# Loads of small parameters moved behind the weights of a decoder's first product

## The chip, the cores and the metric

The kernel runs on one NeuronCore of a Trainium2 chip. The metric is the device time of one execution in microseconds (us). Three timed runs of the kernel before gave 2286.88, 2286.91 and 2288.31 us, a median of 2286.91.

The engines are named as the profile names them: PE is TensorE, PEld its weight loads, ACT ScalarE, DVE VectorE, POOL GpSimd and SP SyncE, which here only asks for transfers (SPq is its queue of instructions). Each engine works through its instructions in their order: one that waits holds back all that stand behind it on that engine. A transfer is asked for by a DMA instruction on some engine; the data are moved by 16 DMA engines, and a semaphore tells the others when they have landed.

## The reference, cut to what matters

The model is a decoder of two layers for 256 tokens of width 2048, in float32. The first layer is an mLSTM mixer and a gated feed-forward block, the second an attention over shared keys and values and another feed-forward block. The part in question is the very start of layer 1:

```python
def rms_norm(x, g):
    xf = x.astype(jnp.float32)
    y = xf * lax.rsqrt(jnp.mean(xf * xf, axis=-1, keepdims=True) + EPS)
    return (y * g.astype(jnp.float32)).astype(x.dtype)
...
def mlstm_mixer(xn, w_in, b_igate, b_fgate, w_hnorm, w_out):
    """xn: normed stream (B,S,D). One combined projection -> q,k,v, output gate, input/forget gates."""
    B, S, _ = xn.shape
    proj = xn @ w_in
    q, k, v, o, ig, fg = jnp.split(proj, M_SPLITS, axis=-1)
...
            h = h + mlstm_mixer(rms_norm(h, a_norm[layer]), m_w_in[layer], m_b_igate[layer],
                                m_b_fgate[layer], m_w_hnorm[layer], m_w_out[layer])
```

`x` is 256 x 2048 and `w_in` is 2048 x 6160. The first 1024 columns of `w_in` give q; the k, v, output gate and gate columns follow. All other products of the model have the same form: 256 tokens against a large weight matrix that is read once.

## The kernel before, in words

Every product is done in three matmuls of a rounded format (fp32r): a float32 operand is split into a high part (a copy on ACT, rounded) and a low part (the difference, on DVE), and high x high, high x low and low x high are summed in PSUM. So every weight tile that lands costs one copy on ACT and one subtraction on DVE before PE can use it. Landed weights lie in one of four buffers (`raw`, RAW = 4), split weights in one of five (`w2`, HL = 5): the copy of a split tile must wait until PE is done with the tile five before it.

The first product, `first_product` (L448), makes q. It goes through the 2048 rows of the weights in 16 chunks of 128 rows, called chunk 0 to 15 here. Chunk k needs 128 x 1024 weights (512 KB) and the 128 columns of x that go with it, turned. A load of x (L458, 256 KB) brings two chunks' columns; the weights of chunks 0 to 3 come one by one (512 KB, L463), and of chunks 4 to 15 in pairs (1 MB). `norm_a.operands(k)` (L202) turns two chunks' columns of x with four PE transposes into one PSUM bank (L207), scales them by the norm's gain and splits them: the high part on ACT (L282), the low part on DVE (L283). These are the operands x_a of chunks k and k + 1. The split of the weights is L478 (ACT) and L479 (DVE), and the 24 matmuls of a chunk are L484. The sums of squares for the norm (L200, ACT) are taken of 512 columns at a time (`SQ_AT` says after which chunks), and the row scale is applied to the products afterwards.

Around it: the norm's gain is loaded and turned first (`columns`, L135 to 149). Eleven small loads of other parameters (L172) and two of gate biases (L174, L175) are asked for by `parameters_in`, which is called when a counter of work pieces has gone 10 on (`later`, L643), held behind the latest weight load by `tc.issue_after`. The convolution's parameters (L144) and rotary tables (L700, L702) belong to the feed-forward block and are written further down (L831 to 834), after most of the output product. All transfers are asked for by SP. After the first product come `gates()` (L510) and the k product (L387), and from there on weights of 1 MB follow each other.

The written order isn't the order that runs. The framework's scheduler places each engine's instructions by its own timeline, and may place a load that is written late far ahead; `tc.issue_after(i)` keeps what is inside it behind instruction i. Semaphores for landed transfers go round: there are eight of them (DMAHW0 to DMAHW7), taken in turn, so a DMA instruction first waits until the transfer eight before it has landed.

Of the kernel before, what the change touches and what calls it, by code (L numbers as in the profile page):

```python
# [19 lines left out]
P = 128  # L20
# [21 lines left out]
X_AT = (0, 2, 3, 5, 6, 8, 9)  # L42
SQ_AT = (3, 6, 9, 12)
CW = 256
# [22 lines left out]
def trunk(  # L67
# [66 lines left out]

    def columns(sources, name):  # L135

        n = sum(s.shape[0] for s in sources)
        cols = const.tile([P, n], F32, name=name)
        at = 0
        for s in sources:  # L140
            for r0 in range(0, s.shape[0], P):
                r = min(P, s.shape[0] - r0)
                rows = work.tile([P, P], F32, tag="rows", name="rows")
                nc.sync.dma_start(rows[:r], s[r0:r0 + r])  # L144
                ps = small_ps("cols_ps")
                pe.transpose(ps[:, :r], rows[:r, :], ident[:r, :r])
                dve.tensor_copy(cols[:, at:at + r], ps[:, :r])
                at += r
        return cols

    gain_a = columns([rows_of(a_norm[0])], "gain_a")
    gate_b = const.tile([40, 1], F32, name="gate_b")
# [15 lines left out]
    def parameter_loads():  # L168
        at = 0
        for a in (rows_of(kv_norm), rows_of(b_norm[0]), rows_of(f_norm[0]), rows_of(f_norm[1]), rows_of(final_norm),  # L170
                  rows_of(m_w_hnorm[0].rearrange("h v -> (h v)")), rows_of(subln[0]), lam_q1, lam_k1, lam_q2, lam_k2):
            nc.sync.dma_start(rows[at:at + a.shape[0]], a)  # L172
            at += a.shape[0]
        nc.sync.dma_start(gate_b[0:8], m_b_igate.rearrange("o h -> h o"))  # L174
        nc.sync.dma_start(gate_b[32:40], m_b_fgate.rearrange("o h -> h o"))  # L175

# [271 lines left out]
    def first_product(evac):  # L448
# [10 lines left out]

        def w_in(k, kc):  # L460
            if k % 2 == 0:
                raw[0] = wpool.tile([P, 2, HQK], F32, tag="raw", name="raw", bufs=RAW)
            loads.append(nc.sync.dma_start(raw[0][:, k % 2:k % 2 + kc], w[k * P:(k + kc) * P, :HQK].rearrange("(k p) n -> p k n", p=P)))  # L463

        x_in(0)
        for k in range(KD):
            if k < 4:
                w_in(k, 1)
            elif k % 2 == 0:
                w_in(k, 2)  # L470
            if k in X_AT:
                x_in(2 + 2 * X_AT.index(k))
            if k % 2 == 0:
                norm_a.operands(k)
            part = raw[0][:, k % 2]
            w2 = wpool.tile([P, 2, HQK], F32R, tag="w2", name="w2", bufs=HL)
            for c in ((slice(0, 512), slice(512, HQK)) if k < 2 else (slice(0, HQK),)):
                act.activation(w2[:, 0, c], part[:, c], AF.Copy)  # L478
                dve.tensor_tensor(w2[:, 1, c], part[:, c], w2[:, 0, c].bitcast(F32), op=ALU.subtract)  # L479
            xh, xl, _ = xs[k]  # L480
            for j in range(n):
                s = slice(j * P, (j + 1) * P)
                for o, (a, b) in enumerate(((w2[:, 0, s], xh), (w2[:, 0, s], xl), (w2[:, 1, s], xh))):
                    pe.matmul(ps[j], a, b, start=(k == 0 and o == 0 and j % 2 == 0), stop=(k == KD - 1 and o == 2), skip_group_check=True)  # L484
            if k + 1 in SQ_AT:
# [7 lines left out]
    def mlstm(norm):  # L493
# [148 lines left out]

        later(10, parameters_in)  # L643
        later(13, parameters)
        first_product(evac_q)
# [184 lines left out]
    convs = []  # L830
    for layer in range(2):  # L831
        cw = columns([rows_of(conv_w[layer, 0]), rows_of(conv_w[layer, 1]), rows_of(conv_w[layer, 2]), rows_of(conv_b[layer])], f"conv{layer}")
        convs.append(cw.rearrange("p (j f) -> p j f", j=4))
    tables = rotary_tables()
    neg_lam = lambda_col()
# [97 lines left out]
```

## Time and profile before

| | us |
|---|---|
| median of three timed runs | 2286.91 |
| profiled execution, its own time | 2288.57 |
| its span, first to last instruction | 2286.8 |
| first matmul of the first product (L484) starts | 8.92 |
| first matmul of the k product (L387) starts | 67.31 |
| PE busy in the span | 2272.3 (99%) |

The profiled execution is 1.77 us longer than its span, and 1.66 us longer than the median of the timed runs. PE is busy nearly the whole time, and the chain of work that ended last is 98% PE. The stretches where PE does not work all lie in the first 36 us.

### The profile page before, as it was taken

Reading aid. Unit: us, or ns where it says so; the run is one execution under the profiler, and the core shown is the slowest. Engines: PE = TensorE matmul, PEld = TensorE weight load, DVE = VectorE, ACT = ScalarE, POOL = GpSimd, SP = SyncE. Lnnn points to the kernel's source line nnn. Section 1 sums busy time; section 2 is a strip of 40 time slices with the busy share of each in tenths; the row PEclk is TensorE's granted clock in tenths of the full one; section 3 lists DMA queues with packets and bytes.
Section 4 is the critical chain, followed back from the end, with each engine's and each line's share of the span. In section 5 each row is a group of like instructions: output and inputs, shape, how many; then the busy total and the mean of one; then the engine's idle time right before and its main releaser. Section 6 shows DMA issues by size and latency. Waiting matters only on the chain.

```text
span 2286.8 us, 31046 instructions
## 1 busy us (share of the span) xinstructions
PE 2272.3 (99%) x12034; PEld 1937.2 (85%) x12034; DVE 1516.2 (66%) x2445; ACT 1209.0 (53%) x1840; POOL 111.2 (5%) x305
## 2 busy tenths in 40 slices
PE   8999999999999999999999999999999999999998
PEld 8878888888888888888888888888888888888887
DVE  5755556777764577775588875557777545777754
ACT  5455554655553455554454556556565434555543
POOL 0013100000000000000022102200000000000000
PEclk9999999999999999999999999999999999999999
DMA  7554555555555555555556555555555555555553
GB/s 255 173 167 160 171 184 185 181 192 186 184 193 184 194 184 187 191 184 193 181 183 188 165 164 168 166 184 185 184 185 190 179 191 195 190 192 188 193 186 118
DMA packets 325192, 418.88 MB, mean 183 GB/s; under 512 B 9054, under 2 KB 238772, under 8 KB 325044
## 3 DMA queue, kind: packets, MB, share of 16 engines
q1 hardware_dynamic: 325044, 416.90, 55.1%
q8 instruction: 94, 1.54, 0.3%
q14 instruction: 54, 0.44, 0.1%
HBM read 414.77 MB, written 2.10 MB: 182 GB/s over the span
## 4 chain that ended last, share of the span: by engine, by line
PE 98%; DMA 1%; SPq 0%; DVE 0%; ACT 0%; issue 0%; DVEq 0%; ACTq 0%
PE acc L387 53%; PE acc L413 40%; PE acc L484 1%; PE val_ps L311 1%; PE acc L431 1%; DMA raw<-in_m_w_in_dram 1%; PE turn_ps L207 0%; DMA stream<-in_x_dram 0%; PE as_ps L768 0%; PE w_ps L593 0%; PE gps L510 0%; PE as_ps L769 0%; PE an_ps L333 0%; PE hn_ps L333 0%; PE s_ps L600 0%; SPq L463 0%
## 5 line engine op out<-in xcount | busy, mean ns | idle before, releaser
L353 DVE TENSOR_TENSOR w<-raw,w 128x1024 fp32r<-128x1024 f32 x768 | 938.6, 1222 | 620.6 <-ACT w L352 619.4
L352 ACT ACTIVATE w<-raw 128x1024 fp32r<-128x1024 f32 x768 | 813.3, 1059 | 790.3 <-PE acc L413 396.1
L387 PE MATMUL acc<-x_f,w 128*128 128x512 f32 (+1 forms) x5632 | 987.5, 337 | 0.0
L387 PEld LDWEIGHTS acc<-x_f,w 128*128 128x128 f32 x5632 | 862.6, 188 | 122.5
L413 PE MATMUL acc<-w,hid 128*128 128x512 f32 (+1 forms) x2112 | 477.7, 388 | 0.0
L413 PEld LDWEIGHTS acc<-w,hid 128*128 128x128 f32 x2112 | 387.3, 188 | 87.5
L413 PE MATMUL acc<-w,x_a 128*128 128x512 f32 x768 | 183.3, 396 | 0.0
L387 PE MATMUL acc<-x_at,w 128*128 128x256 f32 (+1 forms) x1024 | 181.9, 338 | 0.0
L387 PEld LDWEIGHTS acc<-x_at,w 128*128 128x128 f32 x1024 | 156.8, 188 | 22.1
L413 PEld LDWEIGHTS acc<-w,x_a 128*128 128x128 f32 x768 | 142.7, 188 | 32.7
L393 ACT ACTIVATE low<-acc 128x256 f32<-128x256 f32 x216 | 79.5, 385 | 147.2 <-PE acc L387 147.2
L394 DVE TENSOR_TENSOR acc<-acc,low 128x256 f32<-128x256 f32 x216 | 84.8, 432 | 52.2 <-ACT low L393 52.1
L667 ACT ACTIVATE c<-u,conv 128x256 f32<-128x256 f32 x176 | 95.9, 592 | 0.2 <-DVE u L665 0.2
L413 PE MATMUL acc<-w,ao 128*128 128x512 f32 x384 | 92.2, 397 | 0.0
L752 POOL TENSOR_TENSOR sw<-sw,sin_t 32x256 f32<-32x256 f32 x32 | 40.6, 1280 | 1059.7 <-DVE sw L751 1044.6
L413 PE MATMUL acc<-w,x_at 128*128 128x512 f32 x384 | 91.9, 396 | 0.0
L413 PE MATMUL acc<-w,mo 128*128 128x512 f32 x384 | 91.3, 397 | 0.0
L413 PEld LDWEIGHTS acc<-w,mo 128*128 128x128 f32 x384 | 71.4, 188 | 16.5
L413 PEld LDWEIGHTS acc<-w,ao 128*128 128x128 f32 x384 | 71.4, 188 | 16.3
L413 PEld LDWEIGHTS acc<-w,x_at 128*128 128x128 f32 x384 | 71.3, 188 | 16.1
L668 DVE SCALAR_TENSOR_TENSOR c<-u,conv,c 128x255 f32<-128x255 f32 x176 | 77.0, 478 | 0.0
L669 DVE SCALAR_TENSOR_TENSOR c<-u,conv,c 128x254 f32<-128x254 f32 x176 | 76.8, 477 | 0.1
(239 smaller groups left out, 1166.9 us busy)
## 6 DMA issues: line engine op xcount, KB each, us to landing
raw<-in_w_up_dram SPq DMA_DIRECT2D x176, 1024.0 KB
raw<-in_w_down_dram SPq DMA_DIRECT2D x79, 1024.0 KB
raw<-in_m_w_in_dram SPq DMA_DIRECT2D x46, 1024.0 KB
raw<-in_w_kv_dram SPq DMA_DIRECT2D x32, 1024.0 KB
raw<-in_m_w_out_dram SPq DMA_DIRECT2D x16, 1024.0 KB
raw<-in_w_q_dram SPq DMA_DIRECT2D x16, 1024.0 KB
raw<-in_w_o_dram SPq DMA_DIRECT2D x16, 1024.0 KB
raw<-in_w_down_dram SPq DMA_DIRECT2D x15, 512.0 KB
```

The source lines that it names most:

```text
L311: pe.matmul(ps[:, :vh.shape[1]], a, b, start=(s == 0 and o == 0), stop=(s == t and o == 2))
L352: act.activation(w2[:, :hc, 0], part, AF.Copy)
L353: dve.tensor_tensor(w2[:, :hc, 1], part, w2[:, :hc, 0].bitcast(F32), op=ALU.subtract)
L387: pe.matmul(to, a, b, start=(k == 0 and o == 0), stop=(k == kn - 1 and o == len(ops) - 1))
L393: act.activation(low, p[:, T:], AF.Copy)
L394: dve.tensor_tensor(p[:, :T], p[:, :T], low, op=ALU.add)
L413: pe.matmul(ps[t], a[:, s], b, start=(k == 0 and o == 0), stop=(k == kn - 1 and o == 2))
L431: pe.matmul(ps[t], a[:, s], b, start=(k == 0 and o == 0), stop=(k == kn - 1 and o == 2))
L667: act.activation(c, u, AF.Identity, bias=cw[:, 3, f:f + 1], scale=cw[:, 2, f:f + 1])
L668: dve.scalar_tensor_tensor(c[:, 1:], u[:, :T - 1], cw[:, 1, f:f + 1], c[:, 1:], op0=ALU.mult, op1=ALU.add)
L669: dve.scalar_tensor_tensor(c[:, 2:], u[:, :T - 2], cw[:, 0, f:f + 1], c[:, 2:], op0=ALU.mult, op1=ALU.add)
L752: pool.tensor_tensor(sw, sw, sin_t, op=ALU.mult)
```

## The change

Five edits. The gain of the first norm and the weights of chunk 0 are asked for on ACT's queue instead of SP's, the weights in two halves of 512 columns. The four transposes of chunks k and k + 1 are kept behind the last matmul of chunk k - 2. The sums of squares are written after chunks 6, 8, 10 and 12 instead of 3, 6, 9 and 12. The eleven parameter loads go from piece 10 to piece 20 and their transpose from 13 to 25; the two gate biases are apart from them, at piece 11. The convolution's loads and the rotary tables are kept behind the latest weight load. The amount of computation is the same.

```diff
-SQ_AT = (3, 6, 9, 12)
+SQ_AT = (6, 8, 10, 12)
...
-    def columns(sources, name):
+    def columns(sources, name, dma=None):
...
-                nc.sync.dma_start(rows[:r], s[r0:r0 + r])
+                (dma or nc.sync).dma_start(rows[:r], s[r0:r0 + r])
...
-    gain_a = columns([rows_of(a_norm[0])], "gain_a")
+    gain_a = columns([rows_of(a_norm[0])], "gain_a", nc.scalar)
...
+    def gate_biases_in():
+        with tc.issue_after(loads[-1].ins):
+            nc.sync.dma_start(gate_b[0:8], m_b_igate.rearrange("o h -> h o"))
+            nc.sync.dma_start(gate_b[32:40], m_b_fgate.rearrange("o h -> h o"))
...
+        halves = (slice(0, 512), slice(512, HQK))
+        for k in range(KD):
...
+            if k == 0:
+                for c in halves:
+                    w_in(k, 1, nc.scalar, c)
+            elif k < 4:
+                w_in(k, 1, nc.sync)
...
-            if k % 2 == 0:
+            if k == 0:
                 norm_a.operands(k)
+            elif k % 2 == 0:
+                with tc.issue_after(lasts[k - 2].ins):
+                    norm_a.operands(k)
...
+                    last = pe.matmul(ps[j], a, b, start=(k == 0 and o == 0 and j % 2 == 0), stop=(k == KD - 1 and o == 2), skip_group_check=True)
+            lasts.append(last)
...
-        later(10, parameters_in)
-        later(13, parameters)
+        later(11, gate_biases_in)
+        later(20, parameters_in)
+        later(25, parameters)
...
+    with tc.issue_after(loads[-1].ins):
+        for layer in range(2):
+            cw = columns([rows_of(conv_w[layer, 0]), rows_of(conv_w[layer, 1]), rows_of(conv_w[layer, 2]), rows_of(conv_b[layer])], f"conv{layer}")
+            convs.append(cw.rearrange("p (j f) -> p j f", j=4))
+        tables = rotary_tables()
```

What the scheduler makes of it is read from the order of instructions, at three places. A row is line, operation, what it writes <- what it reads, and the size. The lines of the changed kernel are 3 to 14 higher than those of the kernel before (L200 is L203 there, L207 is L210, L282 is L285, L478 is L489, L484 is L495).

The first is the start of ACT. w_169 is the split weights of chunk 0 before, w_199 of chunk 1; in the changed kernel they are w_170 and w_200. Before:

```order
L478 ACT_TABLE_LOAD
L478 ACTIVATE w_169<-raw 128x512 [waits DMAHW2_49]
L478 ACTIVATE w_169<-raw 128x512
L282 ACTIVATE x_a_163<-turn_ps,gain_a 128x256 [waits DVE_49,PE_49]
L200 ACTIVATE sq,parts_a<-stream 128x512 [waits DMAHW3_49,DMAHW1_49]
L200 ACTIVATE sq,parts_a<-stream 128x512
```

In the changed kernel, where DMAHW1 and DMAHW2 are the first two loads of x and DMAHW3 is the first half of chunk 0's weights:

```order
L144 DMA rows<-in_a_norm_dram 16x128
L464 DMA raw<-in_m_w_in_dram 128x512 x2
L203 ACT_TABLE_LOAD [waits DMAHW2_49]
L203 ACTIVATE sq,parts_a<-stream 128x512 [waits DMAHW1_49]
L203 ACTIVATE sq,parts_a<-stream 128x512
L489 ACTIVATE w_170<-raw 128x512 [waits DMAHW3_49]
L285 ACTIVATE x_a_164<-turn_ps,gain_a 128x256 [waits DVE_49,PE_49]
```

The sums of squares over the first two loads of x now stand ahead of the copy of chunk 0's first weights, and a wait for the second load of x stands ahead of ACT's table load.

The second place is SP, from the last three loads of x to the end of the first product's weights. Before:

```order
L458 DMA stream<-in_x_dram 128x2x256 x3
L144 DMA rows<-in_conv_w_dram 88x128 x2
L702 DMA fr<-in_freq_dram 32x2
L463 DMA raw<-in_m_w_in_dram 128x2x1024
L172 DMA rows<-in_kv_norm_dram 16x128
L172 DMA rows<-in_b_norm_dram 16x128
...
L174 DMA gate_b<-in_m_b_igate_dram 8x1
L175 DMA gate_b<-in_m_b_fgate_dram 8x1
L463 DMA raw<-in_m_w_in_dram 128x2x1024 x3
```

In the changed kernel:

```order
L461 DMA stream<-in_x_dram 128x2x256 x3
L464 DMA raw<-in_m_w_in_dram 128x2x1024 x2
L177 DMA gate_b<-in_m_b_igate_dram 8x1
L178 DMA gate_b<-in_m_b_fgate_dram 8x1
L464 DMA raw<-in_m_w_in_dram 128x2x1024 x2
L516 DMA gw<-in_m_w_in_dram 128x16x16
L346 DMA raw<-in_m_w_in_dram 128x8x256 x2
L172 DMA rows<-in_kv_norm_dram 16x128
L172 DMA rows<-in_b_norm_dram 16x128
```

The sixteen small loads that stood between the weights of chunks 6 and 7 and those of chunks 10 and 11 are gone from there; the eleven of L172 stand behind the second load of the k product.

The third place is chunk 10, on PE and on ACT. In the changed kernel x_a_454, x_a_523 and x_a_613 are the operands of chunks 9, 10 and 12, w_529 is the split weights of chunk 10 and w_697 those of chunk 14. On PE:

```order
L495 MATMUL acc<-x_a_454,w_485 128x256 x24
L210 MATMUL turn_ps<-ident,stream 128x128 x4
L495 MATMUL acc<-x_a_523,w_529 128x256 x24
L210 MATMUL turn_ps<-ident,stream 128x128
```

On ACT of the changed kernel:

```order
L489 ACTIVATE w_619<-raw 128x1024
L489 ACTIVATE w_657<-raw 128x1024
L489 ACTIVATE w_697<-raw 128x1024
L285 ACTIVATE x_a_523<-turn_ps,gain_a 128x256
L285 ACTIVATE x_a_526<-turn_ps,gain_a 128x256
```

On ACT of the kernel before, where w_541 is the split weights of chunk 10 and x_a_385 the operand of chunk 7:

```order
L282 ACTIVATE x_a_382<-turn_ps,gain_a 128x256
L478 ACTIVATE w_541<-raw 128x1024
L282 ACTIVATE x_a_385<-turn_ps,gain_a 128x256
L282 ACTIVATE x_a_450<-turn_ps,gain_a 128x256
```

Before, the operand of chunk 7 stood on ACT behind the copy of chunk 10's weights. In the changed kernel the transposes of chunk 10 stand directly ahead of its matmuls, and its operand stands on ACT behind the copy of chunk 14's weights, which takes the buffer of chunk 9's.

## Rows read from the trace of the kernel before

**Rows 1.** The page: busy time and share of each engine, part 1.

```profile
PE 2272.3 (99%) x12034; PEld 1937.2 (85%) x12034; DVE 1516.2 (66%) x2445; ACT 1209.0 (53%) x1840; POOL 111.2 (5%) x305
```

**Rows 2.** The chain of waits from 0 to 200 us: start us, us, what.

```profile
24.82 0.23 SPq L172
...
26.74 6.04 DMA raw<-in_m_w_in_dram
...
67.31 30.29 PE acc L387 x173
```

**Rows 3.** Timeline of PE: start us, us, engine, line, operation xcount [idle before, releaser].

```profile
8.50 0.66 PE L207 MATMUL turn_ps<-ident,stream 128*128 128x128 f32 x4 [3.04 <-DMA stream<-in_x_dram]
8.92 5.08 PE L484 MATMUL acc<-x_a,w 128*128 128x256 f32 x28
...
17.62 10.67 PE L484 MATMUL acc<-x_a,w 128*128 128x256 f32 x88
28.13 1.80 PE L207 MATMUL turn_ps<-ident,stream 128*128 128x128 f32 x15
...
34.34 0.74 PE L484 MATMUL acc<-x_a,w 128*128 128x256 f32 x4 [1.68 <-ACT x_a L282]
35.70 0.50 PE L484 MATMUL acc<-x_a,w 128*128 128x256 f32 x2 [0.62 <-DVE x_a L283]
```

**Rows 4.** Timeline of ACT, 3.9 to 36 us.

```profile
6.73 1.15 ACT L478 ACTIVATE w<-raw 128x512 fp32r<-128x512 f32 x2 [4.74 <-DMA raw<-in_m_w_in_dram]
...
8.54 0.63 ACT L200 ACTIVATE sq<-stream 128x512 bf16<-128x512 f32 x1 [0.29 <-DMA stream<-in_x_dram]
...
9.78 1.14 ACT L478 ACTIVATE w<-raw 128x512 fp32r<-128x512 f32 x2
...
32.87 1.06 ACT L478 ACTIVATE w<-raw 128x1024 fp32r<-128x1024 f32 x1 [3.73 <-DMA raw<-in_m_w_in_dram]
```

**Rows 5.** Timeline of all engines from 0 to 30 us.

```profile
0.71 1.28 ACT L478 ACT_TABLE_LOAD   x1 [0.71 <-PEq L918]
...
1.17 0.41 SPq L458 DMA_DIRECT2D stream<-in_x_dram  x1
...
2.14 0.44 SPq L458 DMA_DIRECT2D stream<-in_x_dram  x1
...
4.35 1.11 PE L207 MATMUL turn_ps<-ident,stream 128*128 128x128 f32 x4
```

**Rows 6.** Timeline of SP at 9.66, 50.84 and 355.27 us; of PE at 389.32.

```profile
9.66 0.37 SPq L458 DMA_DIRECT2D stream<-in_x_dram  x1
...
50.84 3.23 SPq L343 DMA_DIRECT2D raw<-in_m_w_in_dram  x2
...
355.27 0.37 SPq L343 DMA_DIRECT2D raw<-in_m_w_out_dram  x1
...
389.32 0.24 PE L146 MATMUL cols_ps<-ident,rows 88*128 88x88 f32 x1
```

**Rows 7.** Stretches: us, busy (count) by engine, PEclk, DMA share, GB/s.

```profile
3.00:6.00 3.00, 2.46 (x17) 1.83 (x14) 0.57 (x2) 0.00 (x0) 0.32 (x1) 1.00 0.93 217
9.20:12.40 3.20, 3.20 (x17) 3.20 (x17) 1.97 (x4) 3.20 (x8) 0.00 (x0) 0.50 1.05 404
18.00:28.00 10.00, 10.00 (x86) 10.00 (x86) 8.10 (x16) 7.85 (x14) 0.00 (x0) 1.00 0.60 194
36.50:39.80 3.30, 3.30 (x18) 3.30 (x17) 2.79 (x5) 2.08 (x5) 0.00 (x0) 0.50 0.66 133
```

**Rows 8.** Groups by shape, 8.9 to 67.3 us: busy us, mean ns, idle before.

```profile
L479 DVE TENSOR_TENSOR w<-raw,w 128x1024 fp32r<-128x1024 f32 x14 | 16.9, 1223 | 11.5 <-ACT w L478 11.0 <-DMA rows<-in_lam_q_dram 0.4
L478 ACT ACTIVATE w<-raw 128x1024 fp32r<-128x1024 f32 x14 | 14.5, 1055 | 11.2 <-PE acc L484 5.1 <-DMA raw<-in_m_w_in_dram 3.7 <-issue 1.3
L283 DVE SCALAR_TENSOR_TENSOR x_a<-turn_ps,gain_a,x_a 128x256 fp32r<-128x256 f32 x16 | 7.3, 479 | 2.6 <-ACT x_a L282 2.6
L282 ACT ACTIVATE x_a<-turn_ps,gain_a 128x256 fp32r<-128x256 f32 x15 | 6.6, 467 | 5.9 <-PE turn_ps L207 3.2 <-DVE x_a L283 2.7
```

More of the change, by code (lines that the diff above doesn't have):

```diff
@@ L173, in parameter_loads @@
             at += a.shape[0]
-        nc.sync.dma_start(gate_b[0:8], m_b_igate.rearrange("o h -> h o"))
-        nc.sync.dma_start(gate_b[32:40], m_b_fgate.rearrange("o h -> h o"))
+    def gate_biases_in():
+        with tc.issue_after(loads[-1].ins):
+            nc.sync.dma_start(gate_b[0:8], m_b_igate.rearrange("o h -> h o"))
+            nc.sync.dma_start(gate_b[32:40], m_b_fgate.rearrange("o h -> h o"))
     def parameters():
@@ L458, in x_in, with w_in @@
             nc.sync.dma_start(stream[:, :, k * P:(k + 2) * P], x[0, :, k * P:(k + 2) * P].rearrange("(t p) c -> p t c", p=P))
-        def w_in(k, kc):
+        def w_in(k, kc, dma, cols=slice(0, HQK)):
+            loads.append(dma.dma_start(raw[0][:, k % 2:k % 2 + kc, cols], w[k * P:(k + kc) * P, cols].rearrange("(k p) n -> p k n", p=P)))
+        x_in(0)
+        lasts = []
+        halves = (slice(0, 512), slice(512, HQK))
+        for k in range(KD):
             if k % 2 == 0:
                 raw[0] = wpool.tile([P, 2, HQK], F32, tag="raw", name="raw", bufs=RAW)
[L463 to L468, printed above, removed]
+            if k == 0:
[3 more added lines that the diff above has]
+                w_in(k, 1, nc.sync)
             elif k % 2 == 0:
-                w_in(k, 2)
+                w_in(k, 2, nc.sync)
             if k in X_AT:
                 x_in(2 + 2 * X_AT.index(k))
-            if k % 2 == 0:
+            if k == 0:
                 norm_a.operands(k)
+            elif k % 2 == 0:
+                with tc.issue_after(lasts[k - 2].ins):
+                    norm_a.operands(k)
             part = raw[0][:, k % 2]
             w2 = wpool.tile([P, 2, HQK], F32R, tag="w2", name="w2", bufs=HL)
-            for c in ((slice(0, 512), slice(512, HQK)) if k < 2 else (slice(0, HQK),)):
+            for c in (halves if k < 2 else (slice(0, HQK),)):
                 act.activation(w2[:, 0, c], part[:, c], AF.Copy)
@@ L483, in first_product @@
                 for o, (a, b) in enumerate(((w2[:, 0, s], xh), (w2[:, 0, s], xl), (w2[:, 1, s], xh))):
-                    pe.matmul(ps[j], a, b, start=(k == 0 and o == 0 and j % 2 == 0), stop=(k == KD - 1 and o == 2), skip_group_check=True)
+                    last = pe.matmul(ps[j], a, b, start=(k == 0 and o == 0 and j % 2 == 0), stop=(k == KD - 1 and o == 2), skip_group_check=True)
+            lasts.append(last)
             if k + 1 in SQ_AT:
@@ L830, in trunk @@
     convs = []
[L831 to L834, printed above, removed]
+    with tc.issue_after(loads[-1].ins):
[3 more added lines that the diff above has]
+        tables = rotary_tables()
     neg_lam = lambda_col()
```

## The prediction

> **What bounds the kernel now.** I read the page's busy times first, then the chain of waits, then the timelines of PE, ACT and SP over the first product, then stretches with the granted clock. PE is busy 99% of the span [rows 1], so a change helps or harms by the time in which PE stands still or is slow. The reader is to see in the chain that from 67.31 us on, where the k product begins, it runs on PE matmuls [rows 2]. A shift of that moment therefore reaches the end undiminished, and the sum below is of what moves it.
>
> Between the first matmul at 8.92 us and 67.31 PE stands still twice: 1.68 us at 34.34 and 0.62 at 35.70 [rows 3]. The releasers are the operand x_a on ACT and on DVE, but the cause is further back: ACT had sat 3.73 us in the copy of chunk 10's weights [rows 4], behind which the operand of chunk 7 stands in ACT's order. That load was asked for at 26.74 us and took 6.04, after SP had worked through the small parameter loads, one of which had waited until 24.82 for the landing of an earlier load [rows 2]. After each standstill the matmuls are slow as well: at a granted clock of 0.50, the lower level of 1.2 GHz, the stretches 9.2 to 12.4 and 36.5 to 39.8 us hold 17 and 18 PE instructions, while 18 to 28 us at full clock holds 86 [rows 7], which would be 28 in 3.2 to 3.3 us. That is 10 instructions of 10.67 / 88 = 0.12 us [rows 3], 1.2 us each time.
>
> **The change part by part.**
>
> *The small loads leave SP's way.* The load for chunks 10 and 11 is now asked for as soon as its buffer is free. The two standstills (2.3 us) and the slow stretch behind them (1.2) go: -3.5. What is late next on that load is the one before it, landed when SP went on at 24.82 [rows 2]; chunk 10 is needed ten times 24 matmuls of 0.12 us after the first, past 37 us, so nothing shows. The eleven loads now stand on SP ahead of the third load of the k product, which before was asked for at 50.84 us [rows 6]; at 0.23 to 0.41 us each [rows 2, 5] they hold SP for 3 to 5 us. The weights that wait behind them are of the second column group, 64 matmuls into the k product (64 / 173 of 30.29 us [rows 2]), at 78 us. If that cover were gone it would cost those 5 us. The convolution's first rows are asked for behind the twelfth load of the output product; the thirteenth was asked for at 355.27 and PE needs the rows at 389.32 [rows 6], so 34 us hide a landing of a few. Both: nothing.
>
> *ACT's start.* This is the largest term. Before, ACT loads its table at once (1.28 us, at 0.71 [rows 5]), copies chunk 0's weights at 6.73, and takes the sums of squares only at 8.54, when the second load of x has landed [rows 4]. In the new order the wait for that second load stands ahead of the table load, then come two squares, then chunk 0's first half and its operand. After the landing: 1.28 for the table, 9.78 - 8.54 = 1.24 for the squares [rows 4], 0.57 for half of the 1.14 us pair of copies, 0.47 for x_a [rows 8], together 3.56. The landing was at 8.5 before (PE waited for it until 8.50 [rows 3]). It is asked for at SP's second place instead of fourth, so 0.97 earlier (1.17 against 2.14 [rows 5]), but the same megabyte (two loads of x, one chunk of weights) has to pass by then and can begin only 0.45 earlier, a place in SP's queue. I take 8.0. The first matmul then starts at 11.56 instead of 8.92: +2.6. Bounds: if ACT's transfers took nothing from SP's, the landing would follow that of the first load (4.35 [rows 5], less 0.45) by 256 KB at 217 GB/s [rows 7], 1.2 us, at 5.1: -0.3. If it came as late as the weights of chunk 1 now do (9.64, when SP went on [rows 6]), +4.3.
>
> On this the Trainium skill, "DMA: Bandwidth & Descriptors", section "Issuing engines are not separate DMA queues", says that transfers asked for by different engines run on the same 16 DMA engines and interleave, and that several issuers save only the time to issue. By that rule the early bound falls away and the first half gains nothing by standing on ACT's queue; without it, the term could be -0.3 and the sum would be 2.9 us lower. No run here has two issuers yet.
>
> *Work that changes its side.* The second load's four transposes were done before 8.92; now they come after the first matmul: 4 x 1.80 / 15 [rows 3] = +0.5. The third matmul waits for DVE's part of the operand (0.48 [rows 8]) behind its subtraction: +0.25, between 0 and 0.5.
>
> *The slow clock at the start.* It cost 1.2 before; PE had stood still from 5.46 to 8.50 [rows 3, 5]. Now it stands still for six microseconds. If the clock is back at the same moment as before (about 12.5), only 1 us of matmuls is slow: -0.8. If it is slow for a whole stretch more, 1 + 3.4 us at a loss of 1.2 / 3.2 each: +0.4. I take +0.4, the nearer to what the row shows, slow matmuls after work resumes. The Trainium skill, "TensorE: Matmul & The Clock Gate", section "What's actually happening", has the throttled state as the default that activity releases. By that +0.4 holds; the other reading would make the sum 1.2 lower.
>
> *A new wait at chunk 10.* Its transposes stand directly ahead of its matmuls, and its operand on ACT behind the copy of chunk 14's weights, which needs the buffer of chunk 9 and so PE's last matmul of chunk 9. From that matmul on: ACT copies 1.06, then x_a 0.47 [rows 8], with 0.1 taken for signalling 1.63; PE has 0.43 of transposes to do, and waits 1.2. Four matmuls (0.48) follow; DVE needs 1.06 + 0.1 + 1.22 + 0.48 = 2.86 [rows 8], PE is there at 2.11 and waits 0.75. Together +2.0. It is the old pattern (1.68, 0.74 of work, 0.62 [rows 3]) with another copy in front, and it waits for PE's own progress, so early weights don't mend it. Bounds: 1.2 if DVE's part is hidden, 2.1.
>
> *The slow clock behind it.* 2.3 us of standing still were followed by 1.2 us of loss; 2.0 us may or may not be. I take 0.7, between 0 and 1.2.
>
> *Chunk 12.* Three of its four transposes stand directly ahead of it, so PE waits for x_a on ACT: 0.47 and signalling, +0.5, between 0.3 and 0.6. The other chunks have their transposes 24 matmuls (2.9 us) ahead, which covers two copies and an operand on ACT. The squares' new places and the gate biases (two loads of a few bytes) cost nothing, the one beside PE work on an ACT that is busy 53% [rows 1], the other behind loads that run anyway.
>
> **Sum:** -3.5 + 2.6 + 0.5 + 0.25 + 0.4 + 2.0 + 0.7 + 0.5 = +3.45. The profiled execution would go from 2288.57 to 2292.0; it lies 1.66 above the median of 2286.91, on which the forecast stands: 2290.3. With all low bounds: -3.5 - 0.3 + 0.5 + 0 - 0.8 + 1.2 + 0 + 0.3 = -2.6, 2284.3. With all high ones: -3.5 + 4.3 + 0.5 + 0.5 + 0.4 + 2.1 + 1.2 + 0.6 = +6.1, 2293.0.
>
> **Rivals.** A measurement of this kernel can tell 0.2%, 4.6 us, from no change.
>
> *Slower: ACT's queue delays x.* The halves of chunk 0 on a second queue push the second load of x back, and with it table load, squares and first matmul. For it: all of ACT stands behind that landing. Against it: the bytes ahead are no more than before. It decides from a landing after about 9.2 us (+2.6 + 1.2 for it gives +4.6), or after 8.7 if chunk 10's wait also brings the slow clock. At a landing of 9.64, the clock included, the sum is 3.45 + 1.7 + 0.5 = +5.6: 2292.5.
>
> *Faster: the order does not bind as I read it.* If the weights' first half lands with the first load of x and ACT is not held by the squares, the first matmul starts near 6.6 (5.5 for the landing, 0.57, 0.47), 2.3 earlier, and without the waits of chunks 10 and 12 the sum is -3.5 - 2.3 + 0.25 = -5.6: 2281.3. For it: PE is idle from 5.46 to 8.50 [rows 3, 5]. Against it: the wait stands ahead in ACT's order, and ACT takes its instructions in turn.
>
> *The small loads were not the cause.* If the load for chunk 10 came late anyway, the 3.5 would stay and the new wait come on top or merge with it: between +3.5 and +7, about 2292. Against it: SP was at it with small loads from 24.82 to 26.74 while nothing else was asked for [rows 2].
>
> **How the numbers follow.** The forecast, within 0.2%: 0.67. Slower by more: 0.26, of which 0.22 for the delayed x and 0.04 for the last rival. Faster by more: 0.07. The range leaves out the last tenth at each end: 2285.3 to 2292.9.
>
> **What the changed profile would show.** ACT's table load after 7.5 us, right before two squares; first matmul (L495) at 11 to 12; no standstill of PE at chunk 7; the load for chunks 10 and 11 asked for before 20 us; PE waiting for x_a on ACT and then on DVE at chunk 10 near 45 us; the k product starting near 70.8. I am wrong if the table load starts at once, if chunk 10 starts without a wait, or if the k product starts before 67.

## The result, and the profile after

The changed kernel takes 2291.29 us (median of 16 runs, 2289.59 to 2293.63), the kernel before 2287.55 beside it (16 runs, 2286.78 to 2288.88): a ratio of 1.0016, 95% interval 1.0008 to 1.0023. That is +3.74 us: the interval leaves 1 out, so the change costs a little, but it is inside the 0.2% that counts as no change and inside the forecast range; the forecast was 2290.3. The profiled execution took 2289.66, with a span of 2287.9, 1.1 more than the profiled one of before. So the two profiles explain 1.1 us, and the medians differ by 3.7. The second half of this text is mostly about that gap.

The page of the changed kernel answers to [rows 1]: PE is as full as before. (The section "Time and profile before" puts all of PE's standing still in the first 36 us. That holds for its waits; in both kernels PE is also idle for the last 8 us of the span, behind its last matmul, and the change does not touch that end.)

```profile
PE 2271.2 (99%) x12034; PEld 1935.8 (85%) x12034; DVE 1515.8 (66%) x2445; ACT 1209.2 (53%) x1840; POOL 111.3 (5%) x305
```

The chain of waits from 0 to 70 us (start us, us, what), which answers to [rows 2]:

```profile
1.21 5.56 DMA stream<-in_x_dram
...
6.84 1.28 ACT L203
...
42.91 1.06 ACT w L489
...
44.00 1.23 DVE w L490
45.23 0.41 DVE x_a L286
...
52.01 0.48 ACT x_a L285
...
68.37 1.63 PE acc L390 x9
```

No small load stands in it any more. It begins with a landing of x, goes through ACT's table load, and comes back to ACT and DVE at chunk 10 and to ACT at chunk 12. The k product begins at 68.37 where it began at 67.31, +1.06, and that is the whole difference of the two spans. This holds for every profile of this study: from the first matmul of the k product (by the timeline 67.14 before, 68.21 after) to the end of the span it is 2219.6 to 2219.8 us. Below, each kernel is told by that moment.

The timeline of PE of the changed kernel (start us, us, engine, line, operation, count, idle before and its releaser), which answers to [rows 3]:

```profile
10.40 5.56 PE L495 MATMUL acc<-x_a,w 128*128 128x256 f32 x28 [5.43 <-ACT x_a L285]
...
44.39 0.74 PE L495 MATMUL acc<-x_a,w 128*128 128x256 f32 x4 [1.12 <-ACT x_a L285]
45.68 2.56 PE L495 MATMUL acc<-x_a,w 128*128 128x256 f32 x20 [0.55 <-DVE x_a L286]
...
52.54 3.18 PE L495 MATMUL acc<-x_a,w 128*128 128x256 f32 x24 [0.56 <-ACT x_a L285]
```

The first matmul comes 1.48 later, the 28 behind it take 5.56 instead of 5.08; the standstill at chunk 7 is gone, and in its place PE waits 1.12 and 0.55 at chunk 10 and 0.56 at chunk 12, with the releasers that the prediction named. ACT's timeline, to [rows 4, 5], shows why the first matmul is late:

```profile
6.84 1.28 ACT L203 ACT_TABLE_LOAD   x1 [6.84 <-DMA stream<-in_x_dram]
8.14 0.63 ACT L203 ACTIVATE sq<-stream 128x512 bf16<-128x512 f32 x1
...
9.38 0.61 ACT L489 ACTIVATE w<-raw 128x512 fp32r<-128x512 f32 x1
9.90 0.45 ACT L285 ACTIVATE x_a<-turn_ps,gain_a 128x256 fp32r<-128x256 f32 x1
```

The table load now waits for x's second load. From it to the first matmul are 3.56 us, as worked out; but the landing itself was at 6.8 and not at 8.0. SP's timeline, to [rows 6]:

```profile
12.94 3.07 SPq L464 DMA_DIRECT2D raw<-in_m_w_in_dram  x2
...
42.85 0.57 SPq L172 DMA_DIRECT2D rows<-in_kv_norm_dram  x1
...
50.98 0.39 SPq L346 DMA_DIRECT2D raw<-in_m_w_in_dram  x1
```

The load for chunks 10 and 11 is asked for in the second of the two issues that begin at 12.94, more than ten microseconds before 26.74, and the small loads stand at 42.85 without anybody waiting. Last, stretches of the changed kernel (us; busy and count of PE, PEld, DVE, ACT, POOL; granted clock; DMA share; GB/s), to [rows 7]:

```profile
12.00:13.00 1.00, 1.00 (x6) 1.00 (x6) 1.00 (x3) 1.00 (x2) 0.00 (x0) 0.50 1.07 437
...
34.00:38.00 4.00, 4.00 (x36) 4.00 (x35) 2.78 (x10) 2.60 (x4) 0.00 (x0) 1.00 0.29 32
...
44.00:50.00 6.00, 5.06 (x41) 4.85 (x42) 2.80 (x5) 1.87 (x3) 0.00 (x0) 1.00 0.54 174
```

The slow clock at the start is still there; the one at 36 to 40 us is gone; behind the new wait at chunk 10 the clock stayed at its upper level in this execution.

### The profile page after: what moved, and what is told of

It reads as the page before. It is cut to its first block, busy times and chain, and to the rows that moved or that the text cites. A ratio compares the mean times of both kernels' runs of the same rounds, so it can differ in the third digit from the quotient of the medians.

```text
span 2287.9 us, 31052 instructions
## 1 busy us (share of the span) xinstructions
PE 2271.2 (99%) x12034; PEld 1935.8 (85%) x12034; DVE 1515.8 (66%) x2445; ACT 1209.2 (53%) x1840; POOL 111.3 (5%) x305
## 4 chain that ended last, share of the span: by engine, by line
PE 99%; DMA 0%; ACT 0%; DVE 0%; issue 0%; DVEq 0%; SPq 0%; ACTq 0%
PE acc L390 53%; PE acc L416 40%; PE acc L495 2%; PE val_ps L314 1%; PE acc L434 1%; PE turn_ps L210 1%; PE as_ps L781 0%; DMA stream<-in_x_dram 0%; PE w_ps L605 0%; PE gps L522 0%; PE as_ps L782 0%; PE an_ps L336 0%; PE hn_ps L336 0%; PE s_ps L612 0%; PE t_ps L803 0%; PE s_ps L613 0%
```

## The experiments

The kernels were timed in three sets of four, each set on one chip with its own runs of the kernel before: 2288.37 (33 runs) in the first, 2288.34 (33 runs) in the second, 2287.8 (21 runs) in the third. Where kernels of different sets are compared, some tenths of a microsecond may be the chips'. The ratios given with the times were estimated from the runs; they are not the quotients of these medians and differ from them by up to 0.0006.

### The small loads alone

The kernel before with one part of the change: the small loads, the gate biases apart from them, and the convolution's rows move back. Weights, squares and transposes stay as before.

```diff
...
-        later(10, parameters_in)
-        later(13, parameters)
+        later(11, gate_biases_in)
+        later(20, parameters_in)
+        later(25, parameters)
...
```

> The kernel before with one part of the change alone: the small loads moved (parameters, gate biases, convolution and rotary loads), everything else as before. My theory: the small loads cost 2.3 us of standstill at chunk 7 and up to 1.2 us of slow clock behind it. First matmul at 8.9 us as before, no standstill at chunk 7, k product at 64 to 65 us instead of 67.3, time 2.3 to 3.5 us under the kernel before. Rival (the load for chunks 10 and 11 was late anyway): the standstill stays, k product at 67, no gain.

Measured: 2283.96 (11 runs, 2283.43 to 2284.98), ratio 0.9984 [0.9976, 0.9993]. PE's timeline:

```profile
8.75 5.93 PE L487 MATMUL acc<-x_a,w 128*128 128x256 f32 x28
...
30.30 5.71 PE L487 MATMUL acc<-x_a,w 128*128 128x256 f32 x46
...
63.43 2.85 PE L390 MATMUL acc<-x_a,w 128*128 128x512 f32 x15
```

Chunk 7 begins inside the 46 matmuls from 30.30, with no idle time before or in them. The third rival of the prediction (the small loads were not the cause) falls, and this part of the change is worth 4.4 us by itself, more than the 2.3 to 3.5 expected; the k product starts at 63.43, where 64 to 65 was expected. The rest of the change gives back more than it.

### The change without the transposes in turn

```diff
-            if k == 0:
+            if k % 2 == 0:
                 norm_a.operands(k)
-            elif k % 2 == 0:
-                with tc.issue_after(lasts[k - 2].ins):
-                    norm_a.operands(k)
```

> The changed kernel without keeping the transposes in turn (operands(k) for every even k as before); small loads moved and ACT's queue as in the change. My theory: the first matmul stays at about 10.4 us, the waits of chunk 10 (1.1 + 0.55 us) and chunk 12 (0.56) are gone, k product at 66 us in place of 68.4; the time falls by 2.2 us, by more (up to 4) where those waits had brought the slow clock. Rival (only the late start costs, the waits are hidden later): no change from the changed kernel.

Measured: 2286.41 (11 runs, 2285.86 to 2287.86), ratio 0.9995 [0.9986, 1.0004]. PE's timeline:

```profile
7.03 0.78 PE L210 MATMUL turn_ps<-ident,stream 128*128 128x128 f32 x4 [2.11 <-DMA stream<-in_x_dram]
10.62 5.38 PE L492 MATMUL acc<-x_a,w 128*128 128x256 f32 x28 [2.81 <-ACT x_a L285]
...
30.06 1.91 PE L210 MATMUL turn_ps<-ident,stream 128*128 128x128 f32 x16
```

From 10.62 on no wait for an operand is left; the k product starts at 64.77, where 66 was expected. So the two remaining parts of the change can be priced apart: the loads on ACT's queue (the halves and the gain), with what they do to ACT's order and with the squares' new places, which were not timed apart from them, 2286.41 - 2283.96 = +2.45; the transposes in turn 2290.43 (a later run of the changed kernel) to 2291.29 less 2286.41, +4.0 to +4.9.

### The squares held back

The changed kernel, with the sums of squares put behind ACT's copy of two chunks earlier, so that the table load need not wait for x.

```diff
...
-                norm_a.squares(SQ_AT.index(k + 1))
+                with tc.issue_after(copies[k - 2].ins):
+                    norm_a.squares(SQ_AT.index(k + 1))
```

> The changed kernel with each pair of squares held behind the weight copy two chunks earlier on ACT, so that ACT's table load and the copy of chunk 0 no longer stand behind them; the transposes stay in turn. My theory (the order on ACT sets the start): table load at 2 to 3 us, first matmul at 6.5 to 7.5, the waits at chunk 10 and 12 stay; k product about 3 us earlier than in the changed kernel, time 2 to 4 us lower. Rival (two queues that share the DMA engines delay the first weights): table load early, but the first half of chunk 0 lands after 8 us and the first matmul comes at 9 or later.

Measured: 2288.87 (11 runs, 2288.1 to 2289.88), ratio 1.0004 [0.9995, 1.0013]. ACT's timeline:

```profile
2.25 1.28 ACT L489 ACT_TABLE_LOAD   x1 [2.25 <-issue]
7.16 0.63 ACT L489 ACTIVATE w<-raw 128x512 fp32r<-128x512 f32 x1 [3.63 <-DMA raw<-in_m_w_in_dram]
...
8.88 1.15 ACT L489 ACTIVATE w<-raw 128x512 fp32r<-128x512 f32 x2 [0.72 <-DMA raw<-in_m_w_in_dram]
```

The table load is out of the way, some 2 us come back, and the first matmul stands at 8.21. But 6.5 to 7.5 was expected of it, and the k product starts at 66.63, 1.6 before that of the first profile and not 3: the first half lands at 7.16 and the second at 8.88, where the whole chunk in SP's queue landed at 6.73 [rows 4] and 6.63. The halves were not early behind the table load; they were late.

### Both undone

The squares held back and the transposes not in turn; of the change, the small loads and the loads on ACT's queue are left.

```diff
-            if k == 0:
+            if k % 2 == 0:
                 norm_a.operands(k)
...
+                with tc.issue_after(copies[k - 2].ins):
+                    norm_a.squares(SQ_AT.index(k + 1))
```

> The changed kernel with both: squares held behind, transposes not kept in turn. My theory: first matmul near 7.2 us (it needs the second load of x, 6.8 us, whose transposes stand first), no waits at chunks 10 and 12, k product at 62 to 63.5 us, time 4 to 5 us under the kernel before and 7 to 9 under the changed one. Rival (DMA becomes the bound when the product starts earlier): PE waits for weights at chunks 4 to 11 and the k product does not start before 65.

Measured: 2284.51 (11 runs, 2283.36 to 2285.77), ratio 0.9987 [0.9978, 0.9995], k product at 64.27 where 62 to 63.5 was expected. The profiled execution took 2285.77, the slowest time of the eleven. ACT's timeline shows what was late in it:

```profile
8.29 0.63 ACT L486 ACTIVATE w<-raw 128x512 fp32r<-128x512 f32 x1 [4.77 <-DMA raw<-in_m_w_in_dram]
```

In this execution the first half landed as late as 8.29, and x's second load at 7.4. By the medians, asking in halves on a second queue gains nothing over the small loads alone (2283.96).

### Filling PE before the first matmul

The changed kernel with 50 small matmuls behind the first four transposes, for the price of the slow clock at the start.

```diff
                 norm_a.operands(k)
+                fill = small_ps("fill_ps")
+                for _ in range(50):
+                    pe.matmul(fill[:, :P], warm, warm, start=True, stop=True)
```

> The changed kernel, with 50 more small bf16 matmuls on PE behind the first four transposes, so that PE works between 4.9 and about 10 us where it stood idle for 5.43 us; nothing is left out. Theory (the idle before the first matmul is what takes the clock down behind it: 28 matmuls in 5.56 us at a granted clock of 0.50, against 3.3 at full clock): the first 28 take 3.3 to 3.6 us, the k product starts 1.5 to 2.2 us earlier than 68.2, and the time falls by as much. Rival (the clock at the start goes its own way, whatever PE does): the fills run at the lower clock, the first 28 matmuls still take over 5 us, and the time is unchanged. If the fills overrun the first operand, the first matmul comes up to 0.5 us late.

Measured: 2291.99 (11 runs, 2290.42 to 2292.9), ratio 1.0017 [1.0008, 1.0025]. PE's timeline:

```profile
5.26 3.52 PE L485 MATMUL fill_ps<-warm 128*128 128x128 bf16 x50
11.85 0.50 PE L498 MATMUL acc<-x_a,w 128*128 128x256 f32 x2 [3.07 <-ACT x_a L285]
12.61 4.87 PE L498 MATMUL acc<-x_a,w 128*128 128x256 f32 x26 [0.26 <-DVE x_a L286]
```

That is 1.6 above the changed kernel on the same chip, with the k product at 70.53; but it tells little. The fills ran faster than reckoned and ended at 8.78; x's second load landed only at 8.2 in this execution, and PE stood idle for 3.07 us more. From 14 to 15 us the granted clock is 0.50 as ever. The order of the operands moved as well: PE waits 0.56 us at chunk 2, which it did not before. The row does show the wait for DVE's part of the operand, 0.26, that the prediction put at 0.25. The test that it should have been is the ninth run.

### One queue for chunk 0

The changed kernel with chunk 0's weights whole on SP's queue.

```diff
-                for c in halves:
-                    w_in(k, 1, nc.scalar, c)
+                w_in(k, 1, nc.sync)
```

> The changed kernel with chunk 0's weights again asked for whole on SP's queue; the gain's load on ACT's queue, the small loads behind the weights and the transposes in turn stay. Theory (the halves on ACT's queue put the table load and the squares behind x's second load): ACT loads its table near 1 us, chunk 0 lands at 6.6 to 6.8, x's second load near 8.0, first matmul at 8.6 to 8.9. The transposes in turn still cost: one wait for an operand on ACT and then one on DVE, together 1.5 to 2, here at chunk 8, whose operand stands behind the copy of chunk 12's weights, and about 0.5 at chunk 12. Time 2286 to 2287, some 2 above the kernel with the small loads moved alone. Rival (the time of the changed kernel comes from the transposes and their waits alone): first matmul earlier, but the k product still near 68 and the time within 1 us of the changed kernel's.

Measured: 2289.31 (11 runs, 2288.59 to 2291.56), ratio 1.0007 [0.9998, 1.0016]; higher than expected, 1.1 below the changed kernel on the same chip. PE's timeline:

```profile
7.85 5.01 PE L494 MATMUL acc<-x_a,w 128*128 128x256 f32 x24 [2.39 <-ACT x_a L285]
...
30.99 5.43 PE L494 MATMUL acc<-x_a,w 128*128 128x256 f32 x44 [1.19 <-DVE x_a L286]
...
37.98 0.74 PE L494 MATMUL acc<-x_a,w 128*128 128x256 f32 x4 [1.12 <-ACT x_a L285]
39.27 4.16 PE L494 MATMUL acc<-x_a,w 128*128 128x256 f32 x20 [0.55 <-DVE x_a L286]
```

The start is right: chunk 0 lands at 6.29, the first matmul comes at 7.85, 2.5 to 3.4 us before that of the changed kernel. The price of the transposes in turn was put too low. Beside the wait at chunk 8 (1.12 and 0.55, as expected) there is one of 1.19 at chunk 6 (for DVE) and one of 0.56 at chunk 4. And the 20 matmuls behind the wait at chunk 8 take 4.16 us, where the changed kernel's 20 behind a wait of the same length at chunk 10 took 2.56 (here PE had waited 1.19 us seven microseconds earlier, there it had not): from 40 to 42 us the row of the stretch reads

```profile
40.00:42.00 2.00, 2.00 (x11) 2.00 (x11) 0.24 (x1) 0.00 (x0) 0.00 (x0) 0.50 0.29 101
```

Here is the slow clock behind a wait of an operand in turn, 1.6 us of it. This execution took 2291.01; of the eleven, six lie between 2288.59 and 2289.31 and five between 2290.89 and 2291.56, with nothing between, a gap of 1.6. That would fit a clock that falls behind this wait in some executions and not in others; only one of the slower five was profiled, so it is not shown.

### Filling the wait at chunk 10

```diff
                     norm_a.operands(k)
+                    if k == 10:
+                        fill = small_ps("fill_ps")
+                        for _ in range(16):
+                            pe.matmul(fill[:, :P], warm, warm, start=True, stop=True)
```

> The changed kernel, with 16 small bf16 matmuls (about 0.9 us at full clock) on PE between chunk 10's transposes and its first matmul, where PE waited 1.12 us for the operand on ACT; nothing is left out. Theory (in part of the executions that wait takes the clock down behind it, which makes the median of the changed kernel 2.7 us worse than the two profiled executions say): the median falls by 1 to 2.5 us, and the runs lie closer together than the 4 us of the changed kernel's. Rival (the scatter comes from elsewhere): median and scatter as those of the changed kernel, within 0.5 us.

Measured: 2290.96 (11 runs, 2289.41 to 2292.5), ratio 1.0011 [1.0003, 1.002], beside 2290.43 for the changed kernel on that chip. PE's timeline:

```profile
44.42 1.06 PE L489 MATMUL fill_ps<-warm 128*128 128x128 bf16 x16
45.70 0.74 PE L499 MATMUL acc<-x_a,w 128*128 128x256 f32 x4 [0.23 <-ACT x_a L285]
```

The wait is filled but for 0.23, and neither the median nor the scatter (3.1 us, against 3.4) moves. The rival stands as far as it goes: what scatters the changed kernel's times was not removed by this. The wait of 0.55 for DVE was left unfilled.

### The change again

> The changed kernel once more, on the same chip as the three beside it, for their comparison. Theory: 2290 to 2292; in the profile either the k product near 68.2 again, or, where the wait at chunk 10 takes the clock down, a stretch behind 45 us at a granted clock of 0.50 and the k product 1 to 2 us later. Rival (the profile shown is what every execution does): k product within 0.3 us of 68.2 and a median near 2288.7, 1.1 above the kernel before.

Measured: 2290.43 (11 runs, 2289.99 to 2293.42), ratio 1.0015 [1.0006, 1.0024]; the profiled execution took 2290.53, so it is a typical one. Its timelines of ACT and of PE:

```profile
7.65 1.28 ACT L203 ACT_TABLE_LOAD   x1 [7.65 <-DMA stream<-in_x_dram]
```

```profile
11.21 5.71 PE L495 MATMUL acc<-x_a,w 128*128 128x256 f32 x28 [5.74 <-ACT x_a L285]
```

The k product starts at 69.06, and the waits at chunks 10 and 12 are those of the first profile to the hundredth, at the upper clock. What differs is the landing of x's second load, and everything moves with it. The five executions with this beginning have the table load at 6.84 (first profile), 7.06 (without the turns), 7.65 (this run), 8.17 (wait at chunk 10 filled) and 8.29 (start filled), and in each the first matmul comes 3.56 later. Three of them are held up at chunks 10 and 12 and nowhere else; their time less the table load's start is 2282.82 (first profile), 2282.88 (this run) and 2282.79 (wait at chunk 10 filled). Between these three executions, 1.3 us apart, the landing is the whole difference. Both expectations miss a part: the k product is not near 68.2, nor is there a slow stretch behind 45 us.

### Filling PE in the faster kernel

The kernel with the small loads alone, and 40 small matmuls between the transposes of x's first and second load.

```diff
             if k % 2 == 0:
                 norm_a.operands(k)
+            if k == 0:
+                fill = small_ps("fill_ps")
+                for _ in range(40):
+                    pe.matmul(fill[:, :P], warm, warm, start=True, stop=True)
```

> The kernel with only the small loads moved (first run of this study), with 40 more small bf16 matmuls on PE between the transposes of x's first and second load, where PE stood idle for 3.15 us; nothing is left out. 50 such matmuls took 3.52 us in the run with fills in the changed kernel, so these take 2.8 and end just before x's second load lands near 8. Theory (the idle time of PE before the first matmul brings the lower clock behind it; the fills of the earlier run failed because PE then stood idle for 3.07 us more): the first 28 matmuls take 3.3 to 3.6 us instead of 5.93, the k product starts near 61, and the time falls by 1.5 to 2.5 us to about 2282. Rival (the clock falls there whatever PE does): the first 28 take over 5 us again, and the time is within 0.5 us of the kernel without the fills.

Measured: 2282.83 (11 runs, 2282.68 to 2283.66), ratio 0.998 [0.9971, 0.9989]. PE's timeline, and a stretch of it:

```profile
4.79 2.40 PE L481 MATMUL fill_ps<-warm 128*128 128x128 bf16 x40
7.75 0.63 PE L210 MATMUL turn_ps<-ident,stream 128*128 128x128 f32 x4 [0.56 <-DMA stream<-in_x_dram]
8.32 3.95 PE L491 MATMUL acc<-x_a,w 128*128 128x256 f32 x28
```

```profile
10.00:11.00 1.00, 1.00 (x11) 1.00 (x10) 0.95 (x2) 1.00 (x4) 0.00 (x0) 1.00 1.06 425
```

With 0.56 us of idle time left before the second transposes, the clock stays up; the first 28 matmuls take 3.95 us and the k product starts at 61.36. It is the fastest kernel of the study, 5.0 us under the kernel before, and its runs lie closest together. The theory holds in its mechanism; the price is 1.2 us in the medians, under the 1.5 to 2.5 expected.

### The small loads alone, again

> The kernel with only the small loads moved once more, beside its version with the fills and the kernel before on one chip. Theory (the gain is that of the standstill at chunk 7 and of the slow matmuls behind it): 2284 again, 4 to 4.5 us under the kernel before; in the profile no idle time of PE between the first matmul and the k product. Rival (the first measurement was that chip's): a ratio whose interval holds 1.

Measured: 2284.06 (11 runs, 2283.43 to 2284.87), ratio 0.9984 [0.9975, 0.9993], on another chip the same; 3.7 under the kernel before beside it, where 4 to 4.5 was expected, with an interval that leaves 1 out. A line of PE's timeline and a stretch, for comparison with the run above:

```profile
8.36 5.40 PE L487 MATMUL acc<-x_a,w 128*128 128x256 f32 x28
```

```profile
10.00:11.00 1.00, 1.00 (x6) 1.00 (x6) 0.92 (x2) 1.00 (x4) 0.00 (x0) 0.50 1.08 428
```

Six matmuls in that microsecond instead of eleven. The k product starts at 62.51.

### The kernel before, twice

The runs of the kernel before that stood beside the second four: 15 lie between 2286.42 and 2287.28, 18 between 2288.07 and 2290.43, none in the gap. The other sets fall apart in the same way, with 2287.74, 2287.8 and 2287.91 alone in the middle; of the sixteen runs beside the changed kernel eight lie at 2287.14 or below and eight at 2287.96 or above, so that no execution took their median of 2287.55.

> The kernel before once more, for its profile. Its runs fall into two groups, near 2286.8 and near 2288.6; the profile shown earlier is of the upper one (2288.57). Theory: in the lower group the clock stays up behind the standstill at chunk 7, so a run near 2286.8 shows no stretch at 0.50 between 36 and 40 us and its k product starts 1.2 to 2 us earlier than 67.3; a run near 2288.6 looks as the first profile did. Rival: the groups differ in something else, such as the landing of x's second load or the slow stretch at the start, and the stretch at 36 to 40 us is there in both.

> The kernel before a third time, for its profile, with the same two expectations as the run ahead of it: near 2286.8 without a slow stretch between 36 and 40 us by the theory, or near 2288.6 with it; by the rival the difference between the groups lies at the start.

The first came out at 2288.72, the second at 2286.71: one of each group. PE's timeline of the first, then of the second with a stretch:

```profile
34.51 0.73 PE L484 MATMUL acc<-x_a,w 128*128 128x256 f32 x4 [2.02 <-ACT x_a L282]
35.87 18.41 PE L484 MATMUL acc<-x_a,w 128*128 128x256 f32 x140 [0.63 <-DVE x_a L283]
```

```profile
8.60 5.80 PE L484 MATMUL acc<-x_a,w 128*128 128x256 f32 x28
...
34.03 0.73 PE L484 MATMUL acc<-x_a,w 128*128 128x256 f32 x4 [0.98 <-ACT x_a L282]
35.40 16.86 PE L484 MATMUL acc<-x_a,w 128*128 128x256 f32 x140 [0.63 <-DVE x_a L283]
...
65.29 2.96 PE L387 MATMUL acc<-x_a,w 128*128 128x512 f32 x16
```

```profile
37.00:38.00 1.00, 1.00 (x11) 1.00 (x10) 0.56 (x2) 1.00 (x3) 0.00 (x0) 1.00 1.21 131
```

In the execution of the faster group the 140 matmuls behind the standstill take 16.86 us instead of 18.41, at the upper clock, and the standstill is 0.98 instead of 2.02 (1.68 in [rows 3]). The k product starts at 65.29 against 67.32. The theory holds, in one execution of each group. The rival's slow stretch at the start is there too, and in the faster execution it is even the longer one (28 matmuls in 5.80 against 5.08).

## Why the prediction was right

The mechanism was right in which engine waits, for what, and where. The sizes were less so: the slow clock behind chunk 10 did not show, and the first profile is ahead of three forecast times (table load at 6.84, forecast after 7.5; first matmul at 10.40, forecast 11 to 12; k product at 68.2, forecast 70.8). The number was right partly by luck, because two errors cancelled. Term by term, in us, against the first and the typical profile of the changed kernel:

| Step | Forecast | First profile (2289.66) | Second (2290.53) |
|---|---|---|---|
| Small loads: standstill and slow stretch gone | -3.5 | -2.30 - 1.55 | -2.30 - 1.55 |
| ACT's start | +2.6 | +1.48 | +2.29 |
| Slow clock at the start (28 matmuls) | +0.4 | +0.48 | +0.63 |
| Four transposes behind the start | +0.5 | +0.44 | +0.44 |
| DVE's part at the first matmuls | +0.25 | in the 28 above | in the 28 above |
| Wait at chunk 10 | +2.0 | 1.12 + 0.55 | 1.12 + 0.55 |
| Slow clock behind it | +0.7 | 0 | 0 |
| Wait at chunk 12 | +0.5 | 0.56 | 0.56 |
| Sum | +3.45 | +0.78 | +1.74 |
| k product, measured | | +1.07 | +1.92 |

The -1.55 is 16.86 - 18.41, from the two runs of the kernel before; the start and the 28 matmuls are set against 8.92 and 5.08 [rows 3]. The 0.2 to 0.3 us left over are about what one wait more costs beside its idle time (see chunks 10 and 12 below).

*The small loads leave SP's way.* Right: alone it gives -4.4 and, in the last comparison, 2284.06 - 2287.8 = -3.7. Both hang on how the two groups of the kernel before mix in its median: against its faster group, near 2286.8, it is about -2.8, against the slower one, near 2288.6, about -4.6. That nothing would show of the later small loads held too: from the k product to the end all profiles take 2219.6 to 2219.8 us.

*ACT's start.* The largest term, and the order was read rightly: the 3.56 us from landing to first matmul were 3.56 in all five executions. The landing, estimated at 8.0 with bounds of 5.1 and 9.64 (9.66 by [rows 6]), was 6.8 to 8.3 in them; 8.0 is within, toward the late end. Measured as a time, with the clock behind it and the squares' new places, this part cost 2.45. What the prediction drew from the Trainium skill, "DMA: Bandwidth & Descriptors", section "Issuing engines are not separate DMA queues" (transfers of several issuers interleave on the same DMA engines), agrees with the traces: the early bound never came, and the half-chunks landed at 7.16 and 8.29, later than the whole chunk in SP's queue (6.29 to 6.88). The Trainium skill, "Perfetto Trace Analysis", section "DMA Optimizations", says that of a transfer split into smaller chunks some may start sooner, and that the whole may end sooner if the DMA engines are generally idle. No row here shows them idle then: in the first profile of the changed kernel their busy share is 0.92 to 0.98 between 4 and 7 us.

*The slow clock at the start.* Right in size. The ninth run shows that it hangs on PE's idle time before the first matmul: with fills the clock stays at its upper level, without them it falls to 0.50. This agrees with the Trainium skill, "TensorE: Matmul & The Clock Gate", section "What's actually happening", by which activity releases a throttle that is otherwise on.

*Chunks 10 and 12.* 2.23 measured, 2.5 forecast; the pattern, an operand behind a copy that waits for PE's own progress, is where it was expected. Together with the four transposes, DVE's part and the slow clock behind chunk 10 the forecast for the transposes in turn was 3.95, and the medians give 4.0 to 4.9. In both profiles of the changed kernel the clock stayed up there. From the end of the first 28 matmuls to the k product they take 52.4 us (15.80 to 68.21) and 52.3 (16.76 to 69.06), the run without the turns 48.9 (15.84 to 64.77), also at the upper clock: 3.4 to 3.5 us are seen. Of these 2.23 are the waits and 0.44 the four transposes; the rest is about 0.25 at each of the three waits that the idle column leaves out (ahead of a wait, four transposes take 0.60 us, from 42.67 to the start of the idle time; with the next matmul right behind them it starts after 0.36, at 34.07). The rest of the 4.0 to 4.9 is not in these profiles. A later landing of x could add to the median, as it did to the executions with the table load at 7.65 and 8.17; that the clock falls in other executions, as behind such a wait in the run with one queue (1.6 us), would fit too, but no profile of the changed kernel caught it, and filling the wait did not lower the time. What its slowest executions lose (2293.09, 2293.63 and, in the later set, 2293.42, at a mean granted clock of 0.996 where most have 0.998) stays open.

*From the sum to the number: the step that failed.* The sum of +3.45 gave 2292.0, and I then took off 1.66 because the profiled execution lay that much above the median. That was not allowed. The 1.66 is about the distance between the two groups of the kernel before, and by the two later profiles it lies in the very standstill and slow stretch that the change removes. An execution of the faster group has only 0.98 + 0.63 to give back, not 3.85; from it the typical changed execution is 69.06 - 65.29 = +3.77 away, from the slower group +1.92. The sum was some 1.5 too high against the profiled execution, the base 1.66 too low, and 2290.3 came out near 2290.43 and 2291.29 because the two cancel.

*The rivals.* ACT's queue did not delay x: its second load landed at 6.8 to 8.3, and with chunk 0's weights on SP's queue at 7.7 to 8.5 in the six profiles where PE waits for it, and by 7.72 in the run with one queue. The order does bind. The small loads were the cause: moved alone, they take the standstill away.

## What to carry to other kernels

A change of several parts is worth timing in its parts: here one was worth -4.4 us, the other two cost +2.45 and +4 to +5, and only the first should stay. Before a forecast is put on a median, look whether the runs of the kernel fall into groups and which of them the profile is of; a term that belongs to one group must not be taken off the other. Where PE idles before its first product, a few cheap matmuls that last until the operands come can pay: 1.2 us here, and a closer scatter, while asking for the operands in halves on a second queue gained nothing.

## What was not expected of the hardware

- Halves of a 512 KB load on a second queue landed later than the whole on one: 7.16 or 8.29 for the first half, 6.29 to 6.88 for the whole chunk. And the landing of the load beside them varied by 1.5 us between executions (6.8 to 8.3).
- A wait of PE of 1.12 and 0.55 us was followed by 20 matmuls in 2.56 us in one program and in 4.16 in another; a standstill of 0.98 and 0.63 was followed by none that was slow, one of 1.68 and 0.62 by 1.55 us of loss.
- The granted clock can miss a slow stretch: in the faster execution of the kernel before it stands at 1.00 from 8 to 14 us, while the first 28 matmuls from 8.60 took 5.80 us. A matmul takes 415 ns there (9.5 to 12 us), as in the first profile at 0.50, and 281 from 15 to 18 us. The length and the pace of the matmuls show it, the column does not:

```profile
10.00:11.00 1.00, 1.00 (x7) 1.00 (x6) 0.83 (x2) 1.00 (x4) 0.00 (x0) 1.00 1.08 430
```
